# The last store of a batched matmul issued in two halves, with 16 counting instructions in place of 60

## The chip, the cores and the metric

One Trainium2 chip, of which the kernel uses one core. The metric is the time of one execution in device microseconds (us). A run's trace covers the span from the first to the last recorded instruction; the time is about 1.75 us longer than the span.

## The reference

```python
batch, m, k, n = 16, 512, 768, 1024
x: [batch, k, m] float32      y: [batch, k, n] float32
out = np.einsum('bkm,bkn->bmn', x, y)      # [batch, m, n] float32
```

Each batch reads 1.5 MB of x and 3 MB of y and writes 2 MB: 75.5 MB read and 33.6 MB written in all.

## The kernel before

SyncE issues every load and store on one queue. VectorE casts the loaded batch to bf16, TensorE multiplies it in two groups of 24 matmuls (`g` = 0, 1) into two halves of PSUM (the memory that TensorE writes its results to), and ScalarE copies each half to an output buffer `ob`, of which there are five. Stores are issued in bunches, four or more at a time. The parts that matter here:

```python
    def store(b):
        if b < B - 2:
            nc.sync.wait_ge(groups, 2 * (b + 2))
        else:
            nc.sync.wait_ge(outs, b - (B - 3))
        nc.sync.dma_start(o_v[b], ob[b % NO][:]).then_inc(so[b % NO], 16)
    # ... loads of all batches, stores of batches 0 to 14, on SyncE ...

    for _ in range(60):                      # VectorE; nobody waits for idle
        nc.vector.sem_inc(idle, 1)
    # ... casts (VectorE), matmuls (TensorE) ...

    for _ in range(60):                      # ScalarE
        nc.scalar.sem_inc(idle, 1)
    for b in range(B):
        # ... wait for a free ob ...
        for g in range(2):
            nc.scalar.wait_ge(groups, 2 * b + g + 1)
            cp = nc.scalar.copy(ob[b % NO][:, g * HB:(g + 1) * HB]..., ps[g][:])
            if b < B - 1:
                cp.then_inc(room, 1)
        if b == B - 2:
            nc.scalar.drain().then_inc(outs, 1)
    cp.then_inc(outs, 1)
    for b in range(B - NO, B - 2):
        nc.sync.wait_ge(so[b % NO], 16 * (b // NO + 1))
    section.close()                          # a barrier of all engines
    nc.sync.dma_start(o_v[B - 1], ob[(B - 1) % NO][:])     # the last store, 2 MB
```

A partition of `ob` holds 4 rows of the output, 16 KB that are contiguous in memory. Each matmul group fills half of it, 8 KB.

## Time and profile before

| | before |
|---|---|
| time, median of 3 runs | 260.51 us (260.5 to 260.77) |
| span of the profiled run | 258.8 us |
| DMA queue busy, share of 16 engines' span | 98.6% |
| TensorE, VectorE, ScalarE busy | 70%, 32%, 24% |
| DMA rate over the span | 421 GB/s |
| last store issued; landing seen by SyncE | 251.67 us; 258.03 us |

It is read from the queue: the DMA engines have work from 2 us to 251 us without a gap, so no other engine matters in between. Time can be lost only at the start and at the end, and at the end there is a hole of 1.5 us in front of the last store. The prediction below shows the lines.

### The profile page before, as it was taken

To read this page: it belongs to the slowest core of one execution; us is meant where nothing else is said; L and a number is where in the kernel's file an instruction comes from. 1 tells how busy PE (TensorE), PEld (TensorE's weight loads), DVE (VectorE), ACT (ScalarE), POOL (GpSimd) and SP (SyncE) were. 2 spreads that over 40 slices of the span, in tenths; PEclk is the share of its full clock that TensorE was granted. 3 is DMA by queue.
4 is the path that set the end of the run, shared out by engine and by line. 5 is a ranking of instruction groups with operands and counts; after the bars stand their busy time and mean duration, and the time that the engine had idled before them with its cause. 6 is when DMAs were issued, how large, how long until landed. Compare 5 with 4: busy or idle time off the path is not lost. (4 is left out here: it accounts for less than half of the span.)

```text
span 258.8 us, 2506 instructions
## 1 busy us (share of the span) xinstructions
PE 181.6 (70%) x768; PEld 89.3 (34%) x768; DVE 82.0 (32%) x33; ACT 60.9 (24%) x33; POOL 0.2 (0%) x4
## 2 busy tenths in 40 slices
PE   0009999999999006999499920899669980099950
PEld 0004555554545002454145500355325530035520
DVE  0261645527164350011734525002255262300000
ACT  1000442234220005222214002324402200413430
POOL 0000000000000000000000000000000000000000
PEclk9999999999999855899779985699979995569995
DMA  7999989899999999999999989999899999999987
GB/s 273 424 475 410 471 380 479 372 479 395 456 410 441 387 418 430 466 446 418 433 433 425 471 352 443 420 461 479 372 479 403 448 410 390 433 438 420 436 357 324
DMA packets 4514, 109.07 MB, mean 421 GB/s; under 512 B 768, under 2 KB 768, under 8 KB 768
## 3 DMA queue, kind: packets, MB, share of 16 engines
q1 hardware_dynamic: 4512, 109.05, 98.6%
q14 instruction: 2, 0.02, 0.0%
HBM read 75.50 MB, written 33.55 MB: 421 GB/s over the span
## 5 line engine op out<-in xcount | busy, mean ns | idle before, releaser
L157 PE MATMUL ps<-yb,xb 128*128 x768 | 181.6, 402 | 68.0 <-PEq L152 68.0
L157 PEld LDWEIGHTS ps<-yb,xb 128*128 x768 | 89.3, 116 | 159.8 <-issue 89.8
L173 ACT COPY ob<-ps 128x2048 f32<-128x2048 f32 x32 | 59.6, 1872 | 185.3 <-PE ps L157 125.2
L135 DVE CAST yb<-ys 128x6144 bf16<-128x6144 f32 (+1 forms) x17 | 53.8, 3172 | 77.8 <-DMA ys<-in_y_dram 77.8
L131 DVE CAST xb<-xs 128x3072 bf16<-128x3072 f32 x16 | 28.2, 1761 | 62.5 <-DMA xs<-in_x_dram 48.7
L173 ACT ACT_TABLE_LOAD x1 | 1.3, 1283 | 5.3 <-issue 5.3
L203 POOL MEMSET const-bfloat16-1.0<- 128x1 bf16 x1 | 0.1, 103 | 0.0
L203 POOL MEMSET const-uint8-127<- 128x1 uint8 x1 | 0.1, 102 | 0.0
L203 POOL MEMSET const-float32-0.0<- 128x1 f32 x1 | 0.1, 100 | 0.2 <-issue 0.2
L203 POOL MEMSET const-float32-1.0<- 128x1 f32 x1 | 0.1, 99 | 0.0
## 6 DMA issues: line engine op xcount, KB each, us to landing
ys<-in_y_dram SPq DMA_DIRECT2D x16, 3072.0 KB, 18.6
out_dram<-ob SPq DMA_DIRECT2D x16, 2048.0 KB, 27.2
xs<-in_x_dram SPq DMA_DIRECT2D x16, 1536.0 KB, 20.1
```

Source lines behind the costliest of these rows:

```text
L131: nc.vector.tensor_copy(xb[:, i], xs[i][:]).then_inc(cast, 1)
L135: nc.vector.tensor_copy(yb[:, i, ks], ys[i][:, ks]).then_inc(cast, 1)
L157: mm = nc.tensor.matmul(ps[g][:, m, nt], x_w[:, bass.ds(s, 1), kt, mo], yb[:, bass.ds(s, 1), kt, nt * NF:(nt + 1) * NF], start=(kt == 0), ...
L173: cp = nc.scalar.copy(ob[b % NO][:, g * HB:(g + 1) * HB].rearrange("p m (t f) -> p m t f", f=NF), ps[g][:])
L203: nc = _bacc.Bacc("TRN2", target_bir_lowering=False, num_devices=1)
```

## The change

It is meant to fill that hole: the first half of the last store goes out as soon as its PSUM half has been copied, instead of after the second copy and the barrier. The counting instructions only move other instructions in the program.

```diff
 ...
+    nc.sync.wait_ge(outs, 2)
+    nc.sync.dma_start(o_v[B - 1, :, :HB], ob[(B - 1) % NO][:, :HB]).then_inc(last, 16)
-    for _ in range(60):
+    for _ in range(16):
         nc.vector.sem_inc(idle, 1)
 ...
-    for _ in range(60):
+    for _ in range(16):
         nc.scalar.sem_inc(idle, 1)
 ...
             if b < B - 1:
                 cp.then_inc(room, 1)
+            else:
+                cp.then_inc(outs, 1)
 ...
-    cp.then_inc(outs, 1)
 ...
-    nc.sync.dma_start(o_v[B - 1], ob[(B - 1) % NO][:])
+    nc.sync.dma_start(o_v[B - 1, :, HB:], ob[(B - 1) % NO][:, HB:])
```

More of the change, by code (lines that the diff above doesn't have):

```diff
@@ L64 @@
     idle = ec(nc.semaphore("idle"))
+    last = ec(nc.semaphore("last"))
     outs = ec(nc.semaphore("outs"))
```

## The prediction

> **What bounds the kernel now.** I read the whole-span page first, for the DMA rows of the slices. They hold one queue that carries all loads and stores.
>
> ```profile
> PEclk9999999999999855899779985699979995569995
> DMA  7999989899999999999999989999899999999987
> ...
> q1 hardware_dynamic: 4512, 109.05, 98.6%
> ...
> L173 ACT COPY ob<-ps 128x2048 f32<-128x2048 f32 x32 | 59.6, 1872 | 185.3 <-PE ps L157 125.2
> ```
>
> The DMA engines are busy for 98.6% of the 258.8 us span, TensorE for 70%, ScalarE for 24%. The clock dips to 0.5 in places and costs nothing as long as the DMA row stays full. The view of stretches confirms it and shows the rate (columns: stretch, its length, then busy time of PE, PEld, DVE, ACT, POOL, then granted clock, DMA share, GB/s):
>
> ```profile
> 2.00:250.00 248.00, 181.60 (x768) 89.25 (x768) 82.00 (x33) 59.40 (x33) 0.00 (x0) 0.88 1.00 429
> ```
>
> So up to 250 us the time is bytes over bandwidth, and only the two ends can be saved. At the end, in order:
>
> ```profile
> 250.00:251.00 1.00, 0.00 (x0) 0.00 (x0) 0.00 (x0) 1.00 (x1) 0.00 (x0) 1.00 0.80 344
> 251.00:252.00 1.00, 0.00 (x0) 0.00 (x0) 0.00 (x0) 0.48 (x1) 0.00 (x0) 0.98 0.35 148
> 252.00:252.50 0.50, 0.00 (x0) 0.00 (x0) 0.00 (x0) 0.00 (x0) 0.00 (x0) 0.50 0.00 0
> 252.50:257.50 5.00, 0.00 (x0) 0.00 (x0) 0.00 (x0) 0.00 (x0) 0.00 (x0) 0.50 0.99 419
> ```
>
> There is a hole before 252.5 us: the store of batch 14 drains while the last store has not been issued. What holds it back is in the order of time and in SyncE's waits:
>
> ```profile
> 244.49 1.87 ACT L173 COPY ob<-ps 128x2048 f32<-128x2048 f32 x1 [3.37 <-PE ps L157]
> 249.61 1.87 ACT L173 COPY ob<-ps 128x2048 f32<-128x2048 f32 x1 [3.26 <-PE ps L157]
> 251.67 0.33 SPq L188 DMA_DIRECT2D out_dram<-ob  x1
> ```
> ```profile
> SPq L182 <- DMA out_dram<-ob: 6.5, 1, 6.5
> SPq L214 <- DMA out_dram<-ob: 6.0, 1, 6.0
> SPq L47 <- ACTq L47: 1.9, 1, 1.9
> ```
>
> The last two matmul groups are copied out at 244.49-246.36 and 249.61-251.48 us; the section's closing barrier waits for the second copy (1.9 us on ACTq); the 2 MB store is issued at 251.67, and SyncE waits 6.0 us for its landing. All of it then moves with nothing beside it. The first half of its rows had been ready for over 5 us.
>
> **How large the hole really is.** The views sum the DMA packets; the trace records each with start, duration and size, and from those records I took the following. A 16 KB packet takes 0.61 us on its engine, a DMA puts 8 of them on each of 16 engines, and back to back they run without a gap. The engines finish the store of batch 14 one by one: the first at 250.97, fourteen of them by 251.68, the last two at 252.41 and 252.45. On all of them the last store's packets start at 252.50 to 252.65 and end 8 x 0.612 = 4.9 us later, at 257.43 to 257.56. The idle time in the hole sums to 16.3 engine-us, 1.02 us per engine on average, but for the latest engine it is only 0.05 us. That is the crux: the kernel ends when its last engine ends.
>
> The latest engine got its lag early. Instruction fetches ride the same engines:
>
> ```profile
> q1 hardware_dynamic: 17, 0.42, 96.9%
> q14 instruction: 1, 0.01, 1.9%
> ```
>
> This is the DMA view of 10 to 11 us; 8 to 9 us has another. Each is an 8 KB packet of 0.31 us, and the data packet after it is stretched: 1.17 and 1.46 us in place of 0.91. So one engine lost 0.57 and the other 0.86 us. The spread between the first and the last engine to finish a DMA grew from 0.63 us (first load) to 1.04 (second) and is 1.43 at the end. The queue never runs dry in between, so it is never made up. The other late engine gained its 0.6 us from slightly long packets (up to 0.66) after 220 us.
>
> **What the Trainium skill says.** "DMA: Bandwidth & Descriptors", section "Latency and other measured facts", gives about 600 ns from a hardware-generated DMA to its first byte; here issue to first packet is 251.67 to 252.50, 0.83 us with the 0.33 us of the instruction itself. The same page, "Rules for kernel authors", asks for 128 partitions and at least 1 MiB per DMA: each half is 128 rows of 8 KB, exactly 1 MiB, still on all engines; and it says that two transfers to halves serialize on the same engines, so a split is worth only what it fills of the hole. "Runtime: NRT & Kernel Launch", "Instruction fetch mechanics", says that each engine's instructions come in blocks over its own queue, ahead of use; the trace agrees on the queue (q14), but shows 8 KB packets where the page has 16 KiB blocks.
>
> **The change, part by part.**
>
> (1) First half early. It now waits only for the copy that ends at 246.36. With 0.33 us of issue and 0.5 us to the first packet it is in the ring at about 247.2, well before the first engine runs dry at 250.97. Every engine goes straight from batch 14 into it. Its 8 packets of 8 KB I take at 0.309 us each, as the instruction packets show: 2.47 us.
>
> (2) Second half. It is issued where the whole store was, at 251.67 (SyncE's waits on three older stores end at 248.0, the barrier still with the copy at 251.48), so it can start at 252.5. The first engine finishes the first half only at 250.97 + 2.47 = 253.44. So it queues behind, and copy, barrier and issue, about 1 us early, leave the path.
>
> (3) Hence each engine ends at its own dry time plus 16 x 0.309 = 4.94 us, and the two extra things it costs, 128 more packets and 16 semaphore packets of about 0.01 us, are in that. With the old lag: 252.45 + 4.94 = 257.39 against 257.56 before, a gain of 0.15 us. With every engine at the level of the main group (251.68): 256.62, a gain of 0.95.
>
> (4) Counting, 16 for 60 on each of VectorE and ScalarE. In themselves they are free: they run at 67 ns (ScalarE) and 93 ns (VectorE), 4.1 and 5.6 us, ending before the first cast, which starts at 7.18 waiting for its load. But they place the fetches. ScalarE's 64th instruction of the span comes 0.38 us late, a block boundary, and the two fetches follow at 8.97 and 10.91. With 44 fewer, the 64th instruction is what was the 108th: on ScalarE the copy at 244.49, on VectorE the first cast of batch 15 at 212.40. That 0.38 us falls in idle time of both (3.37 us before that copy, and VectorE is far ahead of TensorE there). So the fetches go from about 10 us to about 214 and 247 us. The two engines hit were early ones when they were hit (0.06 and 0.18 us behind the first in the first load), so even with 0.3 to 0.9 us added late they end near the main group. I expect the latest engine to lag less at the end: about 0.7 to 1.2 us behind the first instead of 1.48.
>
> Sum: the end is set by the latest engine, between 250.97 + 0.7 + 4.94 = 256.6 and 250.97 + 1.2 + 4.94 = 257.1, against 257.56: 0.45 to 0.95 us gained. Landing to the end of the span (257.56 to 258.8) and the 1.7 us from span to reported time are untouched.
>
> **Rivals.** *A: the lag stays.* The late engines are late for other reasons, as one of them is; then only 0.15 us is gained, 260.35. For it: the second late engine drifted during stores, unrelated to fetches. Against: it drifted by long packets that came and went.
> *B: the hole is worth its average.* All 1.0 us and a bit more is gained: 259.4. For it: the busy rows average over engines and read like this. Against: the packet ends.
> *C: smaller rows cost.* If a packet of 8 KB had a fixed part of 0.1 us, 16 would cost 1.6 us more and the time would be about 261. Against: 12 KB rows took 0.46 us and 24 KB rows 0.91, nearly proportional.
> *D: a fetch stalls.* If the block had to be waited for at the copy of 244.49 (two to four us), the first half would still be in the ring before 251; on VectorE at 212 there are over ten us of slack before TensorE needs batch 15. About no effect.
>
> **Range and chances.** The middle of 0.45 to 0.95 is 0.7; I shade it to 0.65 for A: 260.51 - 0.65 = 259.86, say 259.9. Low end: B and a little, 259.4. High end: A, 260.4. Runs of before agree within 0.27 us, so this is no wider than needed. 2% would be 5.2 us; the hole in total is 1.5 us long and the tail after 251.67 is 7.1 us, of which 4.9 is moving bytes, so faster by over 2% is all but excluded, and so is slower.
>
> **What would show it.** Step 1: the first half's issue at 246.7 to 247.1 and a DMA share near 1.0 from 250 to 256. Step 2: the second half's issue still at about 251.7, its landing some 5.0 to 5.5 us later in place of 6.3. Step 4: no q14 packet before 200 us and two after; the first y load landing 0.4 us earlier. The prediction is wrong if the DMA share still falls before 252.5, if the 8 KB packets take clearly over 0.31 us, or if the fetches fall at the very end of the program and lengthen its close.

## The result, and the profile after

The changed kernel took 260.54 us (median of 6 runs, 260.49 to 260.65), the kernel before 260.61 us in 6 runs. The ratio is 0.9998, with a 95% interval of 0.9985 to 1.0011: the same. The predicted range of 259.4 to 260.4 missed it.

Lines of the page of the changed kernel, its DMA row in 40 slices and its queues:

```profile
DMA  6999989898999999999999999999899999999996
...
q1 hardware_dynamic: 4656, 109.06, 98.6%
q14 instruction: 2, 0.02, 0.0%
```

The 144 packets more are 128 rows cut in two and 16 semaphore packets. The busy share is the same, and so is the span, 258.8 us.

The order of time at the end of the changed kernel:

```profile
244.51 1.87 ACT L178 COPY ob<-ps 128x2048 f32<-128x2048 f32 x1 [3.67 <-PE ps L162]
246.40 0.33 SPq L125 DMA_DIRECT2D out_dram<-ob  x1
249.32 1.86 ACT L178 COPY ob<-ps 128x2048 f32<-128x2048 f32 x1 [2.95 <-PE ps L162]
251.38 0.33 SPq L194 DMA_DIRECT2D out_dram<-ob  x1
```

The first half is issued at 246.40, as soon as its copy ends, and the second at 251.38, behind copy and barrier. The stretches of the changed kernel (columns as in the prediction: stretch, length, busy time of five engines, clock, DMA share, GB/s) show the hole filled, and then a new tail:

```profile
251.00:252.00 1.00, 0.00 (x0) 0.00 (x0) 0.00 (x0) 0.19 (x1) 0.00 (x0) 0.81 0.89 377
252.00:252.50 0.50, 0.00 (x0) 0.00 (x0) 0.00 (x0) 0.00 (x0) 0.00 (x0) 0.50 1.04 442
252.50:255.50 3.00, 0.00 (x0) 0.00 (x0) 0.00 (x0) 0.00 (x0) 0.00 (x0) 0.50 1.01 429
255.50:256.00 0.50, 0.00 (x0) 0.00 (x0) 0.00 (x0) 0.00 (x0) 0.00 (x0) 0.50 0.85 360
256.00:256.50 0.50, 0.00 (x0) 0.00 (x0) 0.00 (x0) 0.00 (x0) 0.00 (x0) 0.50 0.74 311
256.50:257.00 0.50, 0.00 (x0) 0.00 (x0) 0.00 (x0) 0.00 (x0) 0.00 (x0) 0.50 0.12 49
257.00:257.50 0.50, 0.00 (x0) 0.00 (x0) 0.00 (x0) 0.00 (x0) 0.00 (x0) 0.50 0.04 16
```

The same last stretches of the kernel before:

```profile
256.00:256.50 0.50, 0.00 (x0) 0.00 (x0) 0.00 (x0) 0.00 (x0) 0.00 (x0) 0.50 1.23 524
256.50:257.00 0.50, 0.00 (x0) 0.00 (x0) 0.00 (x0) 0.00 (x0) 0.00 (x0) 0.50 1.23 524
257.00:257.50 0.50, 0.00 (x0) 0.00 (x0) 0.00 (x0) 0.00 (x0) 0.00 (x0) 0.50 0.01 0
```

A packet counts in the stretch in which it starts, so the share can exceed 1. Between 251 and 252.5 us the share rose from 0.35 and 0.00 to 0.89 and 1.04. But where all 16 engines used to start packets up to 257, they now finish one by one: only a share of 0.12 is left after 256.5 and 0.04, less than one engine of 16, after 257. The trace's packet records give the ends. The 16 engines' final packets of the kernel before end between 257.43 and 257.57 us, those of the changed kernel between 255.88 and 257.57. **Fifteen engines finish earlier, most of them by over 0.7 us; the one that decides does not.** SyncE saw the landing at 258.06, against 258.03 before. Its waits after 236 us in the changed kernel (waiter, what it waited for, total, times, longest):

```profile
SPq L220 <- DMA out_dram<-ob: 6.3, 1, 6.3
SPq L125 <- ACT ob L178: 5.2, 1, 5.2
SPq L47 <- ACTq L47: 1.9, 1, 1.9
```

The wait for the second half's landing is 6.3 us, longer than the 6.0 us for the whole store before, although half the bytes were issued: it contains the rest of the first half. The prediction had it 5.0 to 5.5 us from issue to landing; it was 6.7.

The lag of that engine behind the first was 1.68 us when it finished the store of batch 14 (250.98 to 252.66 over the engines), and it kept exactly that lag to the end. The fetches had moved as predicted: none is left before 200 us, the first y load landed at 14.01 in place of 14.49, and the DMA view of 215 to 216 us in the changed kernel has

```profile
q14 instruction: 1, 0.01, 2.0%
```

with the other between 248 and 249 us.

### The profile page after: what moved, and what is told of

Its sections match the earlier page's. It is cut to its first block, busy times and chain, and to the rows that moved or that the text cites. A ratio compares the mean times of both kernels' runs of the same rounds, so it can differ in the third digit from the quotient of the medians.

```text
span 258.8 us, 2419 instructions
## 1 busy us (share of the span) xinstructions
PE 178.6 (69%) x768; PEld 88.8 (34%) x768; DVE 82.0 (32%) x33; ACT 60.9 (24%) x33; POOL 0.2 (0%) x4
## 5 line engine op out<-in xcount | busy, mean ns | idle before, releaser
L162 PE MATMUL ps<-yb,xb 128*128 x768 | 178.6, 397 | 70.7 <-PEq L157 70.6
```

What stands on the lines that cost most here:

```text
L162: mm = nc.tensor.matmul(ps[g][:, m, nt], x_w[:, bass.ds(s, 1), kt, mo], yb[:, bass.ds(s, 1), kt, nt * NF:(nt + 1) * NF], start=(kt == 0), ...
```

## Experiments

All ratios are to the kernel before, timed on the same chip. The last two columns are from the packet records of the profiled run: when the first and the last of the 16 engines finished its final packet.

| run | median us | before us | ratio (95%) | first, last engine done |
|---|---|---|---|---|
| before (first trace) | 260.51 | | | 257.43, 257.57 |
| changed (first trace) | 260.54 | 260.61 | 0.9998 (0.9985 to 1.0011) | 255.88, 257.57 |
| split_60 | 260.81 | 260.74 | 1.0001 (0.9987 to 1.0014) | 256.06, 257.76 |
| whole_16 | 260.69 | 260.74 | 0.9998 (0.9984 to 1.0012) | 257.12, 257.66 |
| rows_17 | 262.98 | 260.74 | 1.0086 (1.0072 to 1.0100) | 257.10, 260.02 |
| rows_16 | 261.59 | 260.74 | 1.0036 (1.0022 to 1.0050) | 257.01, 258.44 |
| split_0 | 261.15 | 260.64 | 1.0019 (1.0005 to 1.0033) | 255.97, 257.66 |
| which_engine (two runs) | 261.04 | 260.64 | 1.0014 (0.9996 to 1.0032) | 256.02, 258.09 |
| records | 261.63 | 260.64 | 1.0037 (1.0023 to 1.0050) | 255.92, 258.43 |
| changed_again | 260.70 | 260.74 | 1.0002 (0.9989 to 1.0015) | 255.99, 257.65 |
| unrolled | 261.10 | 260.74 | 1.0004 (0.9992 to 1.0016) | 256.01, 258.47 |
| split_12 | 260.75 | 260.74 | 1.0002 (0.9989 to 1.0015) | 255.89, 257.66 |
| late_whole | 261.21 | 260.86 | 1.0020 (1.0007 to 1.0034) | 259.15, 259.29 |
| late_split | 260.78 | 260.86 | 1.0002 (0.9988 to 1.0015) | 255.98, 257.49 |

My theory was that the end is set by the DMA engine that lags most (L), and that the split removes only the hole in front of the others. The first question was whether the two parts of the change cancel: a gain from the split, lost again through the moved instruction fetches.

**split_60: the split alone.** Edit of the changed kernel: `range(16)` becomes `range(60)`, twice.

> The store split, but 60 counting instructions as before. Theory L (the end is set by the DMA engine that lags most, and splitting only removes the hole in front of the other engines): the two instruction fetches fall near 9 and 11 us again, one engine carries about 0.86 us of lag from then on, and both it and the engine that drifts during stores are some 1.4 us behind the first at the end; last packet end near 257.4, time 260.3 to 260.6. Rival C (the split gains 0.7 us and the moved fetches lose it again): 259.8 to 260.0.

Measured 260.81 us beside 260.74. There was no gain to be lost, so rival C of this expectation (gain and loss cancel) falls. The fetches were back at 9.18 and 10.95 us, and the lag of the last engine at the end was still 1.70 us. The time is 0.2 us above the expected band; the kernel before stood 0.13 us higher on this chip too.

**whole_16: the counting alone.** Edit of the kernel before: `range(60)` becomes `range(16)`, twice.

> One whole last store as before, but 16 counting instructions. Theory L: the hole before the last store hides the lag up to about 1.5 us, so where the fetches fall does not matter: 260.4 to 260.7, with the DMA share falling to 0 near 252 us. Rival C (the moved fetches cost what the split gains): about 261.2.

Measured 260.69 beside 260.74, so this rival C falls from that side as well. The stretches of this run:

```profile
251.00:252.00 1.00, 0.00 (x0) 0.00 (x0) 0.00 (x0) 0.18 (x1) 0.00 (x0) 0.67 0.39 164
...
256.50:257.00 0.50, 0.00 (x0) 0.00 (x0) 0.00 (x0) 0.00 (x0) 0.00 (x0) 0.50 1.15 492
257.00:257.50 0.50, 0.00 (x0) 0.00 (x0) 0.00 (x0) 0.00 (x0) 0.00 (x0) 0.50 0.09 33
```

The hole is there (0.39), but the last engine fell out of step with the others: it finished batch 14's store at 252.79, 1.82 us behind the first, later than the others could start the last store. It ends at 257.66, where the split kernels' last engine ends too (257.65 and 257.57). With or without the split, the same engine decides at nearly the same moment.

**rows_17 and rows_16: does one engine's lag survive?** Edit of the changed kernel (17, or 16 in the other):

```diff
 ...
         load(b)
+        if b == 1:
+            nc.sync.dma_start(scratch[:17], y_v[0, :17, 0]).then_inc(extra, 16)
 ...
+    nc.sync.wait_ge(extra, 16)
     section.close()
```

Without the final wait, the program could end before the semaphore's last increment.

> The changed kernel with one more load near the start: 17 rows of 4 KB (68 KB) into an unused buffer. 17 has no divisor up to 16 but 1, so by the Trainium skill (DMA: Bandwidth & Descriptors, how many engines) all of it goes over one engine, some 2.6 us of work at 0.155 us for 4 KB. Theory L: nothing makes up for it in 250 us, that engine ends last, and the time grows by 2.6 us plus that engine's own lag (0 to 0.8) less the lag of the engine that was last (1.7): 261.4 to 262.3. Rival E (the engines share the work of the queue, what one loses the others take over): 68 KB over all, under 0.2 us, 260.5 to 260.8.

> The same with 16 rows, 64 KB, one row for each of the 16 engines. Both theories: 0.155 us on every engine, 260.6 to 260.8; it is what rows_17 is compared with.

Both took longer than I expected, by 0.7 to 0.8 us more than the upper end. The packet records of rows_16 say why: each 4 KB packet took only 0.16 to 0.32 us, but the 48 KB packets around it took up to 2.7 us in place of 1.83; a short load inside the stream of long ones cost each engine about 1 us (the first engine finished the later stores 0.9 to 1.1 us later than in the changed kernel's trace). What tells the theories apart is the difference of the two, 1.39 us for one more row. The records of rows_17 show 17 packets of 4 KB one behind the other on one engine. The end of rows_17 in stretches:

```profile
256.00:258.00 2.00, 0.00 (x0) 0.00 (x0) 0.00 (x0) 0.00 (x0) 0.00 (x0) 0.70 0.62 258
258.00:260.00 2.00, 0.00 (x0) 0.00 (x0) 0.00 (x0) 0.00 (x0) 0.00 (x0) 0.50 0.06 25
```

For the last 2 us the share is 0.06, one engine of 16. A lag got at 25 us was still there at 258 us: no other engine takes over its rows. By the records this engine was 3.57 us behind the first at 46 us and 2.91 at the end; the difference is not help from others, for six of them ran dry for 0.06 to 0.44 us at 242 and 255 us. This is shown for this engine and this cause.

**split_0: which lag decides, that of the fetches or that of the drift?** Edit: `range(16)` becomes `range(0)`, twice.

> The store split, no counting instruction at all: the 64th instruction of VectorE and ScalarE then lies behind the last copy, so the two fetches should come at the close of the program or not at all. Theory D (the engine that ends last is the one whose packets are stretched during stores while TensorE works; its drift of 1.4 to 1.7 us needs no fetch): lag at the end still 1.3 to 1.7 us, 260.3 to 260.7. Rival F (a fetch made the last engine late): lag 0.8 to 1.0, 259.8 to 260.0.

The trace has no instruction block of 8 KB left in it, and the lag of the last engine was still 1.69 us. So a fetch is not what makes it last; theory D holds. The span is as before (258.9 us), but the time is 261.15, that is 2.2 us over the span in place of 1.75. So without counting some 0.5 us appear outside the recorded span.

**which_engine: where is the engine that drifts?** Edit: before the store of batch 13, three loads of 8 rows of 2 KB, 4 rows of 1 KB and 2 rows of 768 bytes; the section waits for their semaphore.

> The changed kernel with three small loads before the store of batch 13, of 8 rows of 2 KB, 4 rows of 1 KB and 2 rows of 768 bytes, which by the Trainium skill run on the lowest 8, 4 and 2 engines. The packets mark the engines: the one that drifts can be placed among 0-1, 2-3, 4-7 or 8-15. No theory of the time; up to 1.5 us longer, as in rows_16.

The engine with the largest lag started its 2 KB packet at 243.18 us, 1.87 us behind the first, and had none of 1 KB or 768 bytes: by the rule that the expectation names (the lowest-numbered engines, the same section as for rows_17) it is one of engines 4 to 7. The engine that the fetch had delayed had a 1 KB packet and none of 768 bytes: 2 or 3. So they are two engines. (Only two runs, 261.04 us; whether the loads cost time here, they can't say.)

**records: what makes that engine drift?** In the packet records its drift appears only during stores, and only while TensorE works: between 220 and 225 us, with 4 instructions starting, the 16 KB packets together are stretched by 0 ns; between 225 and 240 us, with 172 instructions, by 377 ns, nearly all on one engine. During loads there is none, save some 0.1 us in the first two behind a bunch of stores. Edit of the changed kernel:

```diff
             nc.gpsimd.wait_ge(cast, nx[b] + h + 1).then_inc(ready, 2 // parts(b))
+    with nc.Fori(0, 24, engines=OrderedEngineSet([nc.gpsimd.engine])):
+        for _ in range(8):
+            nc.gpsimd.sem_inc(idle, 1)
```

> The changed kernel with a loop of 24 x 8 counting instructions on GpSimd after its last wait, from about 222 us on, which touch no data: about 190 to 270 more instructions (with the loop's own) beside the 285 that the trace shows from 225 to 250 us. Theory I (the stretch of one engine's packets comes with instructions being executed or recorded, of whatever kind): the drift of 0.7 us in that stretch grows by 0.4 to 0.7 us, the time to 260.9 to 261.2. Theory T (it comes with TensorE's own traffic): drift 0.7 us as before, 260.5 to 260.7.

Measured 261.63 us, about 1 us more, above even the band of theory I; theory T falls. In 225 to 240 us 353 instructions started and the stretch was 984 ns: 2.8 ns for each, against 377 / 172 = 2.2 before. From 220 to 225 us, where TensorE doesn't yet work, this run has 40 instructions and 119 ns of stretch, where the changed kernel has 4 and none. So the stretch needs no work of TensorE. The end of this run:

```profile
256.50:257.00 0.50, 0.00 (x0) 0.00 (x0) 0.00 (x0) 0.00 (x0) 0.00 (x0) 0.50 0.20 82
257.00:257.50 0.50, 0.00 (x0) 0.00 (x0) 0.00 (x0) 0.00 (x0) 0.00 (x0) 0.50 0.04 16
257.50:258.00 0.50, 0.00 (x0) 0.00 (x0) 0.00 (x0) 0.00 (x0) 0.00 (x0) 0.50 0.08 33
258.00:258.50 0.50, 0.00 (x0) 0.00 (x0) 0.00 (x0) 0.00 (x0) 0.00 (x0) 0.50 0.04 16
```

One engine runs on alone for over a microsecond, with a lag of 2.51 us. Instructions that move no data made the kernel slower, by making one DMA engine's packets longer. By which path they do that, the runs don't show. Every run here was recorded, the timed ones too, so it may be the writing of the records itself; that stays open.

**changed_again and unrolled: fewer instructions.** The first is the changed kernel unedited. The second writes out TensorE's inner loop over the two buffers:

```diff
-        with nc.Fori(0, 2, engines=pe) as s:
+        for s in range(2):
 ...
-    x_w[:, bass.ds(s, 1), kt, mo], yb[:, bass.ds(s, 1), kt, ...]
+    x_w[:, s, kt, mo], yb[:, s, kt, ...]
```

> The changed kernel itself, to stand beside the two others on the same chip: 260.4 to 260.8, lag of the last engine about 1.7 us, as before.

> The changed kernel with TensorE's inner loop over the two buffers written out, so that the 480 register operations that compute their addresses are gone, with the same matmuls and loads of weights. Theory I (each executed instruction during a store stretches one engine's packets by about 2.5 ns): some 30 of 140 instructions a batch fewer, the drift over all stores falls from 1.4-1.7 to 1.1-1.4 us, the time by about 0.3 us to 260.2 to 260.4, unless the longer loop body makes TensorE fetch instructions in the loop, which would show as q14 packets. Theory T (the stretch is TensorE's data traffic): no change.

changed_again came out as expected: 260.70, lag 1.66. In unrolled the stretch fell to 216 ns for 106 instructions in 225 to 240 us (2.0 ns each), beside 384 ns for 170 in changed_again: as theory I says. The time did not follow. Its six runs lie in two groups, 260.34 and 260.50, and 261.07 to 261.37. In the profiled one, of the upper group, an instruction block holds one DMA engine up. Its page has a line that no other run's page has:

```profile
q8 instruction: 1, 0.02, 0.0%
```

The record behind it is one packet of 16 KB at 40.09 us that took 1.08 us; the 48 KB packet after it took 2.31 us in place of 1.83. The engine kept a lag of 2.6 us behind the first from there. The expectation had named such a fetch, of TensorE's longer loop, as what could undo the gain. The records don't say whose block it was, and since only one of the six runs has a trace, that the two groups come from it is not shown. As a better kernel this attempt failed: median 261.10.

**split_12: the counting again.** Edit: 12 in place of 16, twice.

> The changed kernel with 12 counting instructions: the block boundary of ScalarE then falls on what was its 112th instruction, a barrier step of the close, in place of the last but one copy. Theory P (crossing the boundary stalls its engine about 0.38 us, hidden beside idle time but not in the close; with no counting it fell behind the recorded span and cost 0.5 us): span or time 0.3 to 0.6 us longer than the changed kernel, 260.9 to 261.2, and no ScalarE fetch before 258 us. Rival N (the 0.5 us of split_0 had another cause, such as the early start of ScalarE's table load): 260.4 to 260.7.

Measured 260.75, as the changed kernel: my expectation was wrong. The two fetches came at 252.68 and 253.61 us, where VectorE and ScalarE had only the end left to wait for, and on two DMA engines that were not the last, so I take the stall to be hidden. This doesn't prove rival N; where the 0.5 us of split_0 come from stays open. What is shown is only that 12, 16 and 60 are equal and 0 is worse.

**late_whole and late_split: when would the split pay?** The edit is the same in the kernel before and in the changed one:

```diff
+            if (b, g) == (B - 1, 1):
+                nc.scalar.copy(xs[0][:, :4].rearrange("p (m t) f -> p m t f", t=NT), ps[g][:])
             cp = nc.scalar.copy(ob[b % NO][...], ps[g][:])
```

A first form, which copied twice to the same place, was a race.

> The kernel before with a throwaway copy of the last PSUM half (1.87 us on ScalarE, into a load buffer no longer read) ahead of the last real copy, which makes the last store's issue 1.87 us later. Theory L (a store split pays what the hole exceeds the lag of the last engine): the hole grows from about 1.5 to 3.4 us on the first engine, the last engine waits about 1.8 us, the time grows by 1.6 to 1.9 us to 262.2 to 262.6.

> The changed kernel with the same throwaway copy. Theory L: the second half is in the ring at about 254.1, the last engine ends the first half only at about 255.1, so the late issue is hidden from it: 260.4 to 260.8, the same as without the copy and 1.6 to 1.9 us below late_whole. Rival G (copy, barrier and issue still set the end in the split kernel): about 262.4, as late_whole.

The order of time in late_whole:

```profile
249.56 1.86 ACT L174 COPY xs<-ps 128x2048 f32<-128x2048 f32 x1 [3.26 <-PE ps L157]
251.32 1.87 ACT L175 COPY ob<-ps 128x2048 f32<-128x2048 f32 x1
253.39 0.33 SPq L190 DMA_DIRECT2D out_dram<-ob  x1
```

And in late_split:

```profile
248.56 1.87 ACT L179 COPY xs<-ps 128x2048 f32<-128x2048 f32 x1 [2.94 <-PE ps L162]
250.32 1.87 ACT L180 COPY ob<-ps 128x2048 f32<-128x2048 f32 x1
252.38 0.33 SPq L196 DMA_DIRECT2D out_dram<-ob  x1
```

late_split took 260.78 us (260.53 to 261.00), as if the extra copy weren't there; rival G falls. late_whole took 261.05 to 262.31, median 261.21. Its profiled run is the slowest, 262.31, and there the account fits: the last engine was through with batch 14 at 252.70 and all engines start the last store at 254.22, 0.83 us after the issue, and end at 259.29. The median is 1 us below my band. I had taken the end of TensorE's work as fixed, but it moves between runs: the throwaway copy starts at 249.56 in this trace and at 248.56 in that of late_split. With the store whole, the end should follow that, and with it split, it should not; the four other runs of late_whole have no trace to show it. The mean of all five runs is 261.51 against 260.76 us, 0.75 us apart, but that leans on the profiled run. The two ratios, which leave the profiled runs out, are 0.0018 apart, or 0.47 us, and their intervals overlap a little. So the split is worth some 0.5 us here, with an uncertainty of about the same size, where nothing was seen of it before.

## Why the prediction was wrong, point by point

- **"What bounds the kernel now" held.** The queue sets the time up to 251 us, and the crux that the prediction named, that the kernel ends when its last engine ends, is what the runs show: rows_17 and records moved one engine's end and the time with it.
- **Parts (1) and (2) held.** The first half was issued at 246.40, 0.3 us or more before what I wrote, the share was 0.89 or more from 251 to 255.5 us, and the second half, issued at 251.38, queued behind the first. (The skill's rule on two transfers, which the prediction quotes, speaks of halves of the partitions, and here each half has all 128. The records show the same: 8 packets of each half on every one of the 16 engines, the second half behind the first.)
- **Part (3) held, its term for packets included.** Each engine needed 4.90 us from the end of batch 14's store to its own end (250.98 to 255.88), where I had 4.94. Rival C of the prediction, a fixed cost for smaller rows, falls with it.
- **Part (4) held where it placed the fetches** (packets at 215.36 and 248.25 us; 214 and 247 predicted) **and failed in what it drew from them.** "I expect the latest engine to lag less at the end: about 0.7 to 1.2 us behind the first instead of 1.48." It lagged 1.68. The fetches did what was expected: the engine of the first ended 1.21 us behind. But it wasn't the last. The last was the engine that drifts during stores. Both ends of the prediction's sum, 250.97 + 0.7 + 4.94 and 250.97 + 1.2 + 4.94, leave it out. Followed packet by packet, it was the last one in the trace before too, at 252.45, and the engine of the fetches ended at 252.41; the prediction had called the latest engine one that "got its lag early".
- **The failing step** is thus the treatment of the second late engine, under rival A: "it drifted by long packets that came and went". I had seen its drift in the trace before, read it as 0.6 us after 220 us and took it for chance. Added up over that trace, the stores have 1.26 us of such stretch, 0.54 of it in batches 0 to 7. It is systematic: in every kernel traced some packets of one engine were stretched during stores while instructions ran, at 2.0 to 2.8 ns for each instruction that started, in records more with more instructions. In the sum, this lag had been 1.48 us before (252.45 less 250.97) and was 1.68 after, 0.20 us more, which used up the 0.15 us left to gain. With 250.98 + 1.68 + 4.90 the last engine ends at 257.56, just where the last one ended before. Rival A is what happened. Whether its 0.15 us is there, the runs can't tell: the interval of the ratio is 0.34 us to either side, and with the same split store the lag was 1.50 us in one trace (late_split) and 1.70 in another (split_60).
- **The counting was free,** as part (4) said, at 16 and 12; at 0 it was not (0.5 us outside the span), which the prediction didn't foresee.

## What to carry to other kernels

Before filling a hole in the DMA row, look at when each engine runs dry and not at the mean: the hole here was 1.02 us per engine on average, and only 0.05 to 0.2 us for the engine that was through with batch 14 last (the records don't name engines, so which of the starts from 252.50 to 252.65 is its own stays open). Rows given to one engine stayed with it here (the 17 of rows_17), so in a queue that never runs dry a small delay of one engine is carried to the end. A split last store does make the end independent of a late last copy (some 0.5 us in the late pair), so it is worth having where the copy, the barrier and the issue come later than the slowest engine.

## What the Trainium skill lacked or had wrong

- "DMA: Bandwidth & Descriptors" ("Why a DMA increments its semaphore by 16 and not by 1") says that the engines of a DMA finish independently, but not that their lag lasts: it was 1.43 to 2.91 us in the split kernels at the end of these runs, and one engine's extra load of 68 KB at 25 us was still to be seen at 260 us. Its rule for how many engines a DMA uses agrees: 17 rows ran on one engine, 16 rows on 16.
- No page has that executed instructions lengthen the store packets of one DMA engine, by 2.0 to 2.8 ns for each (377 ns for 172, 984 ns for 353, 216 ns for 106), an engine among 4 to 7 here. Whether it is so without recording, no run shows.
- "Runtime: NRT & Kernel Launch", "Instruction fetch mechanics", speaks of 16 KiB blocks and a cost that is mostly hidden. One block in these traces came as a packet of 16 KB (unrolled, q8), those that the counting moves as packets of 8 KB (q14). Each of 8 KB held up its DMA engine by 0.42 to 0.98 us (0.31 to 0.33 us for itself, the rest in a longer packet behind it) and the one of 16 KB by 1.56 us (1.08 for itself), which a full queue never gave back.
- "DMA: Bandwidth & Descriptors" ("Rules for kernel authors") has transfers under 64 KB as mostly overhead, which reads as a cost of their own; here one of 64 KB, just at that bound, with 4 KB per engine between packets of 48 KB, cost about 1 us on every engine, though its own packet took 0.16 to 0.32 us.
